# Elementwise steps of a mixer on VectorE and ScalarE in place of GpSimd, and a planner that models the port

## The chip, the cores and the metric

The kernel runs on one core of a Trainium2 chip. The core has a matrix engine (TensorE, PE in the profile; its weight loads are PEld), three elementwise engines (VectorE = DVE, ScalarE = ACT, GpSimd = POOL) and SyncE (SP), which here issues all DMAs. The metric is the device time of one execution in microseconds, the median of several runs.

## The reference

Two layers work on one sequence of 256 tokens by 1024 channels, all in float32. Each layer adds four blocks to x, every one with a norm ahead and a norm behind: a half-weighted SwiGLU feed-forward, a mixer of three branches, a cross-attention into 256 memory tokens, and a second half-weighted feed-forward.

```python
for l in range(DEPTH):
    x = x + 0.5 * _rmsnorm(_swiglu(_rmsnorm(x, ng[0]), w_ffn_in[l, 0], w_ffn_out[l, 0]), ng[1])
    y = _mixer_block(_rmsnorm(x, ng[2]), cos, sin, ...)
    x = x + _rmsnorm(y, ng[3])
    y = _mem_attn(_rmsnorm(x, ng[4]), _rmsnorm(mem, mem_norm[l]), ...)
    x = x + _rmsnorm(y, ng[5])
    x = x + 0.5 * _rmsnorm(_swiglu(_rmsnorm(x, ng[6]), w_ffn_in[l, 1], w_ffn_out[l, 1]), ng[7])
```

The mixer projects its input once, runs causal latent attention with a rotary part (`_mla_branch`), gated linear attention (`_gla_branch`) and RWKV-7 (`_rwkv_branch`), multiplies each branch's projection by a sigmoid gate, adds the three and projects the sum:

```python
merged = gates[:, :, 0] * y_a + gates[:, :, 1] * y_b + gates[:, :, 2] * y_c
return merged @ w_out
```

## The kernel before

**Products in three passes.** The large matmuls use a split of float32: a weight chunk of 128 x 512 is loaded by DMA into one of three `raw` buffers, ScalarE copies its high part into one of eight `whi` buffers, VectorE subtracts to get the low part into `wlo` (`split`), and TensorE makes three products (`mm3`) of high and low parts. The activations are split in the same way into the heap `heapr`. So each weight chunk needs one ScalarE and one VectorE instruction before TensorE can use it. Results gather in eight PSUM banks, two each of `b_g`, `b_ya`, `b_yb` and `b_s`.

**An order that a planner writes.** The program is first recorded as a list of operations (`Program.add`). `order` then plans it: each operation has a cost in us by its engine and shape (`cost`), each dependency a lag, and `forward` goes through the engines in simulated time and takes for each the ready operation of the lowest rank. `backward` derives new ranks from the plan's times, and this is repeated four times; the whole recording is repeated six times with buffers placed by the previous plan's times, and the plan with the shortest simulated span is issued. So a new cost or a new rule in `forward` can change the order of every engine's queue in every part of the kernel, and where buffers lie. On the chip each engine runs its queue strictly in the issued order.

`forward` charges tensor operations a drain when the size of the used part of the array changes (`part` gives the size and place of each matmul's part), and charges half the cost to every second one of the matmuls in a row on different parts of the same size. It knows nothing of an exclusion between VectorE and GpSimd.

**Where GpSimd works.** All of these go through `tt` with GpSimd as engine, or call it directly:

- `rwkv_keys` and `rwkv_products`: 12 products of 128 x 256 a layer, between the projections and the first matmuls of the RWKV chunks.
- `rwkv_front`: four copies of 64 x 256 of the identity into the matrix `MM`, for each half of the tokens.
- `mla_up`: the rotary steps of queries and keys (`rope`), six small steps each, for each half.
- `gla_attend`: a loop over seven levels (chunks of 64, 32, ... 1) and a last step. Each level subtracts on VectorE, takes the exponential on ScalarE, multiplies the key half (128 x 256) and twice the query half into the matrix `zq` (64 x 256 each), and then TensorE multiplies the two; the result goes into the attention matrix by a copy of ScalarE or a predicated copy of VectorE. At the end come two products of 128 x 512 for each half, with the norm's gain and the gate.
- `rwkv_out`: two products or sums with the norm's weight and bias and one with the bonus, 128 x 512, for each half.
- `branch`: four sums of 128 x 512 into the merged result for each of the second and third branches.
- Norms (`meansq`, `rstd`): a scale-and-add and a power, on 128 x 1 to 128 x 8; they stay there. In `ffn` GpSimd also multiplies the gain vector by 0.5.

The triangular solve (`rwkv_solve`) runs on VectorE, 62 small steps in a row for each half, and then goes out to DRAM and back through the buffers `sx` and `si` before `rwkv_back` can start on TensorE. The second half's solve is recorded just ahead of `gla_attend`, and the planner interleaves the two.

Of the kernel before, what the change touches and what calls it, by code (L numbers as in the profile page):

```python
# [16 lines left out]
AF = mybir.ActivationFunctionType  # L17
# [10 lines left out]
EPS = 1e-6  # L28
# [20 lines left out]
class Program:  # L49
# [138 lines left out]

    @staticmethod
    def columns(op):  # L190
        if op[1] == "transpose":
            return op[2][1].shape[0] * np.prod(op[2][1].shape[1:]) / 128
        x = op[3]["rhs"]
        return x.shape[0] * np.prod(x.shape[1:]) * (1 if x.dtype == F32R else 4) / 128
# [6 lines left out]
    def order(self):  # L201

        self.preds = self.graph()
        ops = self.ops
        n = len(ops)
        self.eng = [o[0].name for o in ops]
        self.costs = [self.cost(o) for o in ops]
        self.succ = [[] for _ in range(n)]
        for i, p in enumerate(self.preds):
            for j in p:  # L210
                self.succ[j].append(i)
        self.size = [o[2][0].nbytes() / self.DMA_RATE if o[0].name == "sync" else 0.0 for o in ops]
        self.cols = [self.columns(o) if o[0].name == "tensor" else 0.0 for o in ops]
        self.parts = [self.part(o) for o in ops]
        rank, rest = [0.0] * n, 0.0
        for i in range(n - 1, -1, -1):
            rank[i] = -self.costs[i] + min((rank[s] - self.lag(i, s) for s in self.succ[i]), default=0.0)
        for i in range(n - 1, -1, -1):
            rest += self.costs[i] if self.eng[i] == "tensor" else 0.0
            rank[i] -= self.ALPHA * rest  # L220
        best = None
        for _ in range(self.ROUNDS):
            span, at, order = self.forward(rank)
            if best is None or span < best[0]:
                best = (span, at, order)
            rank = self.backward(at)
        self.span, self.at, order = best
        for i, users in enumerate(self.users):
            t = self.at[i]
            for b in users:  # L230
                b.start, b.end = min(b.start, t[0]), max(b.end, t[1] + (4.0 if self.eng[i] == "sync" else 0.2))
        return order
# [41 lines left out]
    def forward(self, rank):  # L274
# [12 lines left out]
        at = [None] * n  # L287
        parts, size, place, shared = self.parts, (128, 128), None, False
        while len(order) < n:
            best = None  # L290
            for e in names:
# [4 lines left out]
                if t is not None and (best is None or t < best[0]):  # L296
                    best = (t, e)
            t, e = best
            while wait[e] and wait[e][0][0] <= t:
                i = heapq.heappop(wait[e])[1]  # L300
                heapq.heappush(ready[e], (rank[i], i))
# [11 lines left out]
            if e == "tensor":  # L313
                while recent and recent[0][0] < t - self.TICK:
                    recent.popleft()
                if cols[i] < 1500 * cost[i] and sum(x[1] for x in recent) + cols[i] < self.KEEP:
                    j = min((x for x in ready[e] if cols[x[1]] >= 1500 * cost[x[1]]), default=None)
                    if j:
# [3 lines left out]
                        i = j[1]  # L322
                if parts[i][0] != size:
                    j = min((x for x in ready[e] if parts[x[1]][0] == size and x[0] < rank[i] + self.STAY), default=None)
                    if j:
                        ready[e].remove(j)
                        heapq.heapify(ready[e])
                        heapq.heappush(ready[e], (rank[i], i))
                        i = j[1]
                recent.append((t + cost[i], cols[i]))  # L330
            c = cost[i]
            if e == "tensor":
                if parts[i][0] != size:
                    size, shared = parts[i][0], False
                    c += self.DRAIN
                elif size != (128, 128) and not shared and any(
                        a != b for a, b, s in zip(parts[i][1], place, size) if s < 128):
                    shared = True
                    c *= 0.5
                else:  # L340
                    shared = False
                place = parts[i][1]
# [5 lines left out]
            if e == "tensor":  # L348
# [4 lines left out]
                columns += cols[i]  # L353
                c *= 1 if warm else 2
            at[i] = (t, t + c)
            free[e] = t + c
# [89 lines left out]
class Trunk:  # L446
# [369 lines left out]

    def meansq(self, halves, jk, ss):

        for hf in range(2):
            self.act(jk[:, hf * 512:hf * 512 + 512], halves[hf], AF.Square, scale=1.0 / 32, accum_out=ss[:, hf:hf + 1])  # L820
        g = self.nc.gpsimd
        g.tensor_scalar(ss[:, 0:1], ss[:, 0:1], ss[:, 1:2], EPS, ADD, ADD)
        g.tensor_tensor(ss[:, 0:1], ss[:, 0:1], self.mhalf, ALU.pow)
# [19 lines left out]

    def postnorm(self, y, gb, t):

        jk, yg, ss = self.h.alloc(D), self.h.alloc(D), self.sm.alloc(2)
        self.meansq(y, jk, ss)
        for hf, c in enumerate(self.halves):
# [12 lines left out]
    def ffn(self, l, i, st, post_g, nxt, after_first=None):  # L861
# [46 lines left out]
        for c in range(1, NCH):  # L908
# [3 lines left out]
            if c == NCH - 4:  # L912
                gb = self.gain(post_g)
                self.nc.gpsimd.tensor_scalar(gb.ap, gb.ap, 0.5, 1.0, MULT, MULT)
                nxt(None)
# [10 lines left out]
        for t in range(2):  # L926
            for hf in range(2):
                mms(t, hf, NCH - 2, w9)
                mms(t, hf, NCH - 1, w10)
            self.postnorm(ys[t], gb, t)  # L930
            nxt(t)
# [70 lines left out]
    def rwkv_keys(self, l):  # L1002
# [34 lines left out]
        for hp in range(4):  # L1037
            self.tt(kmv[:, hp, :], kmv[:, hp, :], k0[:, hp, :], MULT, nc.gpsimd)
        h.free(self.k0)
        for hp in range(4):  # L1040
            self.tt(aa[:, hp, :], aa[:, hp, :], kv[:, hp, :], MULT, nc.gpsimd)

    def rwkv_products(self, l):
# [5 lines left out]
        for hp in range(4):  # L1049
            self.tt(rv[:, hp, :], self.rr.v(f, b=4)[:, hp, :], self.km.v(f, b=4)[:, hp, :], MULT, nc.gpsimd)  # L1050
        self.bon = self.sm.alloc(16)
# [32 lines left out]
    def rwkv_front(self, l, t):  # L1084
# [6 lines left out]
        mm5 = MM.v("p (c h e n) -> p c h e n", c=2, h=4, e=2)  # L1091
        for u in range(0, 16, 4):
            nc.gpsimd.tensor_copy(MM.v("p (u n) -> p u n", n=128)[0:64, u:u + 4, 0:64],
                                  self.ident[0:64, 0:64].unsqueeze(1).to_broadcast([64, 4, 64]))
        for e in range(2):
# [153 lines left out]
    def rwkv_out(self, l, och, ocl):  # L1249
# [7 lines left out]
        for t in range(2):  # L1257
# [10 lines left out]
            self.tt(y, y, s.ap.unsqueeze(2).to_broadcast([128, 8, 64]), MULT)  # L1268
            self.tt(Y.ap, Y.ap, lw, MULT, nc.gpsimd)
            self.tt(Y.ap, Y.ap, lb, ADD, nc.gpsimd)  # L1270
            bo = self.bon[:, t * 8:t * 8 + 8]
            vn = VN.v(v8, h=8)
            self.tt(vn, vn, bo.unsqueeze(2).to_broadcast([128, 8, 64]), MULT)
            self.tt(Y.ap, Y.ap, VN.ap, ADD, nc.gpsimd)
            ps = self.bank("ya")
# [13 lines left out]

    def rope(self, dst, x1, x2, t, n, eng):  # L1290
        h = self.h
# [4 lines left out]
        for j, (a, b) in enumerate(((x1, c), (x2, s), (x1, s), (x2, c))):  # L1296
            self.tt(tv[:, j], a, b, MULT, eng)
        self.tt(dst[:, :, 0:16], tv[:, 0], tv[:, 1], SUB, eng)
        self.tt(dst[:, :, 16:32], tv[:, 2], tv[:, 3], ADD, eng)
        h.free(T)  # L1300
# [40 lines left out]
    def mla_up(self, l):  # L1341
# [6 lines left out]
        for t in range(2):  # L1348
# [6 lines left out]
            q = qn[t].v(q3, h=8)  # L1355
            self.rope(q[:, :, 64:96], q[:, :, 64:80], q[:, :, 80:96], t, 8, nc.gpsimd)
        wk = self.wload([(0, self.kview(self.w["mla_w_ukv"][l]))], True)[0]
        pr = self.bank("s")[0:32, 0:256]
        for t in range(2):
            kr = sm.alloc(32)  # L1360
            cr = c0[t].ap
            self.rope(kr.ap.unsqueeze(1), cr[:, 384:400].unsqueeze(1), cr[:, 400:416].unsqueeze(1), t, 1, nc.gpsimd)
            self.tr(pr[:, t * 128:t * 128 + 128], kr.ap)
# [98 lines left out]
    def gla_attend(self, l, obh, obl):  # L1462
# [48 lines left out]
        for i, L in enumerate((64, 32, 16, 8, 4, 2, 1)):  # L1511
# [8 lines left out]
            self.act(T.ap, T.ap, AF.Exp)  # L1520
            self.tt(tv[:, :, 0, :], tv[:, :, 0, :], kv[:, :, 0, :], MULT, nc.gpsimd)
            upat = "p (u b x n) -> p u b x n"
            tq, qq = (b.v(upat, u=4, x=2, n=L)[:, :, :, 1, :] for b in (T, QG))
            by_head(Z, lambda pe, z: self.tt(z.rearrange("p u (b n) -> p u b n", n=L), tq[pe], qq[pe], MULT, nc.gpsimd))
            ps = self.bank("yb", (4, 128))
# [7 lines left out]
            else:  # L1533
# [8 lines left out]
        self.act(T.ap, T.ap, AF.Exp)  # L1542
        self.tt(t2[:, :, 0:128], t2[:, :, 0:128], kg[:, :, 0:128], MULT, nc.gpsimd)
        by_head(Z, lambda pe, z: self.tt(z.rearrange("p (h x) n -> p h x n", h=2),
                                         t2[pe, :, 128:256].rearrange("p h (x n) -> p h x n", x=2),
                                         qg[pe, :, 128:256].rearrange("p h (x n) -> p h x n", x=2), MULT, nc.gpsimd))
        ps = self.bank("yb", (2, 256))
# [5 lines left out]
        for t in range(2):  # L1553
# [12 lines left out]
            self.tt(ov, ps, ss.ap.unsqueeze(2).to_broadcast([128, 4, 128]), MULT)  # L1566
            self.tt(ov, ov, self.p_gn.unsqueeze(1).to_broadcast([128, 4, 128]), MULT, nc.gpsimd)
            self.tt(O.ap, O.ap, gg[t].ap, MULT, nc.gpsimd)
            pt = self.bank("yb", (4, 128))
# [13 lines left out]
    def mixer(self, l, st, post_g, nxt):  # L1583
# [33 lines left out]
        def branch(i, o, gt):  # L1617
            for ch in range(2):
                cc = slice(ch * 512, ch * 512 + 512)

                def consume(t, ps):
                    self.tt(gt[t][:, cc], gt[t][:, cc], ps, MULT)
                    if i:
                        self.tt(mg[t][:, cc], mg[t][:, cc], gt[t][:, cc], ADD, nc.gpsimd)

# [216 lines left out]
```

## Time and profile before

| what | value |
|---|---|
| time, median of 3 runs | 1686.76 us (1681.28 to 1687.56) |
| the profiled execution | 1683.41 us, its span 1681.7 us |
| VectorE busy | 1105.1 us |
| ScalarE busy | 964.1 us |
| GpSimd busy | 268.4 us in 383 instructions |
| granted TensorE clock, mean | 0.983 |

Almost every instruction stands on one line of the kernel, that of `issue`, so groups are told apart by their tiles: `b_g` and so on for the PSUM banks, `raw`, `whi` and `wlo` for weight chunks, `heap` and `heapr` for the activations, `small` for norm factors, `zq` for the query half of a GLA level. Spans of an engine are the times from start to end of an instruction, so an instruction that is held up by another engine at the memory shows as a long one, not as idle time. "Idle before" is the time that an engine waited ahead of a group, with who ended the wait.

### The profile page before, as it was taken

The numbers are of one execution on the slowest core, as the hardware profiler recorded it, in microseconds if no ns is written. First come the engines' busy times: TensorE is split into PE (matmuls) and PEld (weight loads), VectorE is DVE, ScalarE is ACT, GpSimd is POOL, SyncE is SP. The second block draws the span as 40 slices with busy tenths as digits, with TensorE's granted clock in tenths as the row PEclk, the third lists the DMA queues.
The fourth block names the chain that finished last, engine by engine and source line by source line (L and its number), as shares of the span: only waits on it lengthen the run. The fifth ranks groups of instructions, "written<-read, shape, count | busy, mean of one in ns | idle before, by whom it ended". The sixth has DMA issues, their size and how long they took to land. (4 is left out here: it accounts for less than half of the span.)

```text
span 1681.7 us, 23946 instructions
## 1 busy us (share of the span) xinstructions
PE 1602.7 (95%) x8623; PEld 1337.0 (80%) x8623; DVE 1105.1 (66%) x1954; ACT 964.1 (57%) x1887; POOL 268.4 (16%) x383
## 2 busy tenths in 40 slices
PE   7999999998899999999999999999978999999998
PEld 5788798776677987888878887887766789878886
DVE  5555656958876667555675557676786776575555
ACT  5455675866445556555555556867854455564544
POOL 7000113105331101000010002310163320010000
PEclk9999999999999999999999999999988999999999
DMA  8655542522555635656555554443225555455652
GB/s 253 207 190 186 171 155 88 169 73 103 170 192 180 206 128 163 202 173 214 174 180 199 193 182 146 131 143 115 91 83 173 175 188 165 149 169 182 199 177 100
DMA packets 206091, 274.91 MB, mean 163 GB/s; under 512 B 28148, under 2 KB 157650, under 8 KB 205972
## 3 DMA queue, kind: packets, MB, share of 16 engines
q1 hardware_dynamic: 205972, 273.39, 50.0%
q8 instruction: 67, 1.10, 0.3%
q14 instruction: 52, 0.43, 0.1%
HBM read 270.60 MB, written 2.75 MB: 163 GB/s over the span
## 5 line engine op out<-in xcount | busy, mean ns | idle before, releaser
L384 DVE TENSOR_TENSOR wlo<-raw,whi 128x512 fp32r<-128x512 f32 (+1 forms) x964 | 673.5, 714 | 401.1 <-ACT whi L384 389.7
L384 ACT CAST whi<-raw 128x512 fp32r<-128x512 f32 (+1 forms) x964 | 582.4, 619 | 484.7 <-PE b_g L384 256.8
L384 PE MATMUL b_g<-whi,heapr 128*128 128x512 f32 (+2 forms) x1904 | 656.3, 405 | 15.8 <-DVE heap L384 5.5
L384 PEld LDWEIGHTS b_g<-whi,heapr 128*128 128x128 f32 x1904 | 357.4, 191 | 97.6 <-DVE heapr L384 7.3
L384 PE MATMUL b_g<-wlo,heapr 128*128 128x512 f32 (+2 forms) x952 | 369.3, 403 | 0.5 <-DVE wlo L384 0.4
L384 PEld LDWEIGHTS b_g<-wlo,heapr 128*128 128x128 f32 x952 | 181.5, 191 | 36.6 <-DVE wlo L384 2.3
L384 PE MATMUL b_g<-heapr,whi 128*128 128x256 f32 x1104 | 201.6, 290 | 2.8 <-DVE heap L384 2.8
L384 POOL TENSOR_SCALAR small<-small 128x1 f32<-128x1 f32 (+2 forms) x52 | 30.3, 583 | 987.4 <-ACT heap L384 962.7
L384 PE MATMUL b_ya<-whi,heapr 128*128 128x512 f32 x480 | 178.0, 394 | 0.2 <-ACT heapr L384 0.2
L384 PE MATMUL b_yb<-whi,heapr 128*128 128x512 f32 x480 | 174.6, 392 | 0.0
L384 PE MATMUL b_s<-whi,heapr 128*128 128x512 f32 x448 | 174.5, 399 | 0.0
L384 PEld LDWEIGHTS b_g<-heapr,whi 128*128 128x128 f32 x1104 | 166.2, 193 | 6.5 <-DVE heap L384 4.0
L384 POOL TENSOR_TENSOR heap<-heap 128x256 f32<-128x256 f32 (+2 forms) x85 | 101.8, 1208 | 207.7 <-DVE heap L384 105.5
L384 PE MATMUL b_g<-heapr,wlo 128*128 128x256 f32 x552 | 134.9, 290 | 0.0
L384 DVE TENSOR_TENSOR heap<-heap 128x512 f32<-128x512 f32 (+31 forms) x296 | 116.6, 406 | 15.8 <-PE b_yb L384 8.8
L384 PEld LDWEIGHTS b_yb<-whi,heapr 128*128 128x128 f32 x480 | 89.8, 188 | 18.9 <-DVE heapr L384 0.2
L384 PEld LDWEIGHTS b_ya<-whi,heapr 128*128 128x128 f32 x480 | 89.3, 188 | 19.2 <-ACT heapr L384 0.4
L384 PE MATMUL b_s<-ident,heap 128*128 128x128 f32 (+2 forms) x449 | 92.7, 275 | 10.1 <-DVE heap L384 8.4
L384 ACT CAST heapr<-b_s 128x256 fp32r<-128x256 f32 (+2 forms) x148 | 65.5, 444 | 58.2 <-PE b_s L384 50.8
L384 PEld LDWEIGHTS b_s<-whi,heapr 128*128 128x128 f32 x448 | 83.6, 188 | 18.4 <-DVE heap L384 0.6
L384 PEld LDWEIGHTS b_g<-heapr,wlo 128*128 128x128 f32 x552 | 96.2, 193 | 1.7 <-issue 1.0
L384 DVE TENSOR_TENSOR heapr<-b_s,heapr 128x256 fp32r<-128x256 f32 (+2 forms) x148 | 75.3, 509 | 33.6 <-ACT heapr L384 33.1
(163 smaller groups left out, 1692.3 us busy)
## 6 DMA issues: line engine op xcount, KB each, us to landing
raw<-in_w_ffn_in_dram SPq DMA_DIRECT2D x172, 512.0 KB, 4.9
raw<-in_w_in_dram SPq DMA_DIRECT2D x50, 1024.0 KB, 5.0
raw<-in_w_ffn_out_dram SPq DMA_DIRECT2D x44, 1024.0 KB, 6.9
raw<-in_mem_wkv_dram SPq DMA_DIRECT2D x16, 1024.0 KB, 6.0
raw<-in_w_branch_dram SPq DMA_DIRECT2D x12, 1024.0 KB, 5.3
raw<-in_w_out_dram SPq DMA_DIRECT2D x8, 1024.0 KB, 5.0
raw<-in_mem_wq_dram SPq DMA_DIRECT2D x8, 1024.0 KB, 4.8
raw<-in_mem_wo_dram SPq DMA_DIRECT2D x8, 1024.0 KB
```

The costliest lines, as they stand in the source:

```text
L384: getattr(eng.real, method)(*a, **k)
```

## The change

The products and sums listed above leave GpSimd for VectorE, by dropping the engine argument (`rope` loses its parameter). The four identity copies of `rwkv_front` become one ScalarE copy of 64 x 1024. The halving of the feed-forward's norm is done inside the norm: the root mean square is taken of twice the values (`over=2`), so that its inverse is half as large, and the multiplication of the gain falls away. In the planner, `shared` marks the operations that read SBUF through what VectorE and GpSimd share, and `forward` lets neither run on it while the other holds it; and for matmuls on parts of the array it prefers one on another place than the last, and charges half the cost to every one on another place.

```diff
     @staticmethod
+    def shared(op):
+
+        eng, method, a, k = op
+        if eng.name not in ("vector", "gpsimd") or method in ("memset", "iota"):
+            return False
+        out = k["out"] if "out" in k else a[0]
+        ins = [x for x in list(a) + list(k.values()) if isinstance(x, bass.AP) and x is not out and x.space != PSUM]
+        ins = [x for x in ins if int(np.prod(x.shape[1:])) > 1]
+        return len(ins) >= (2 if eng.name == "vector" else 1) or eng.name == "gpsimd"
...
+        held = dict(vector=0.0, gpsimd=0.0)
...
+            if e == "gpsimd" and t < held["vector"]:
+                free[e] = held["vector"] + 0.03
+                continue
...
-                if parts[i][0] != size:
-                    j = min((x for x in ready[e] if parts[x[1]][0] == size and x[0] < rank[i] + self.STAY), default=None)
+                if parts[i][0] != size or size != (128, 128) and parts[i][1] == place:
+                    some = [x for x in ready[e] if parts[x[1]][0] == size and x[0] < rank[i] + self.STAY]
+                    j = min((x for x in some if parts[x[1]][1] != place), default=None)
+                    if not j and parts[i][0] != size:
+                        j = min(some, default=None)
...
-                elif size != (128, 128) and not shared and any(
-                        a != b for a, b, s in zip(parts[i][1], place, size) if s < 128):
-                    shared = True
+                elif place != parts[i][1]:
                     c *= 0.5
...
+            if e == "vector" and self.port[i]:
+                t = max(t, held["gpsimd"])
+            if e in held and self.port[i]:
+                held[e] = t + c
...
-    def meansq(self, halves, jk, ss):
+    def meansq(self, halves, jk, ss, over=1):
...
-            self.act(jk[:, hf * 512:hf * 512 + 512], halves[hf], AF.Square, scale=1.0 / 32, accum_out=ss[:, hf:hf + 1])
+            self.act(jk[:, hf * 512:hf * 512 + 512], halves[hf], AF.Square, scale=over / 32, accum_out=ss[:, hf:hf + 1])
...
-        g.tensor_scalar(ss[:, 0:1], ss[:, 0:1], ss[:, 1:2], EPS, ADD, ADD)
+        g.tensor_scalar(ss[:, 0:1], ss[:, 0:1], ss[:, 1:2], EPS * over * over, ADD, ADD)
...
-                self.nc.gpsimd.tensor_scalar(gb.ap, gb.ap, 0.5, 1.0, MULT, MULT)
...
-        for u in range(0, 16, 4):
-            nc.gpsimd.tensor_copy(MM.v("p (u n) -> p u n", n=128)[0:64, u:u + 4, 0:64],
-                                  self.ident[0:64, 0:64].unsqueeze(1).to_broadcast([64, 4, 64]))
+        nc.scalar.copy(MM.v("p (u n) -> p u n", n=128)[0:64, :, 0:64], self.ident[0:64, 0:64].unsqueeze(1).to_broadcast([64, 16, 64]))
...
-            self.tt(Y.ap, Y.ap, lw, MULT, nc.gpsimd)
-            self.tt(Y.ap, Y.ap, lb, ADD, nc.gpsimd)
+            self.tt(Y.ap, Y.ap, lw, MULT)
+            self.tt(Y.ap, Y.ap, lb, ADD)
...
-            self.tt(tv[:, :, 0, :], tv[:, :, 0, :], kv[:, :, 0, :], MULT, nc.gpsimd)
+            self.tt(tv[:, :, 0, :], tv[:, :, 0, :], kv[:, :, 0, :], MULT)
...
-            by_head(Z, lambda pe, z: self.tt(z.rearrange("p u (b n) -> p u b n", n=L), tq[pe], qq[pe], MULT, nc.gpsimd))
+            by_head(Z, lambda pe, z: self.tt(z.rearrange("p u (b n) -> p u b n", n=L), tq[pe], qq[pe], MULT))
...
-                        self.tt(mg[t][:, cc], mg[t][:, cc], gt[t][:, cc], ADD, nc.gpsimd)
+                        self.tt(mg[t][:, cc], mg[t][:, cc], gt[t][:, cc], ADD)
```

The other places (`rwkv_keys`, `rwkv_products`, `rope` and its callers, the last step and the end of `gla_attend`, the third step of `rwkv_out`) change in the same way.

More of the change, by code (lines that the diff above doesn't have):

```diff
@@ L189, in columns @@
     @staticmethod
+    def shared(op):
[6 more added lines that the diff above has]
+        return len(ins) >= (2 if eng.name == "vector" else 1) or eng.name == "gpsimd"
+    @staticmethod
     def columns(op):
@@ L214, in order @@
         self.parts = [self.part(o) for o in ops]
+        self.port = [self.shared(o) for o in ops]
         rank, rest = [0.0] * n, 0.0
@@ L287, in forward @@
         at = [None] * n
-        parts, size, place, shared = self.parts, (128, 128), None, False
+        parts, size, place = self.parts, (128, 128), None
+        held = dict(vector=0.0, gpsimd=0.0)
         while len(order) < n:
@@ L333, in forward @@
                 if parts[i][0] != size:
-                    size, shared = parts[i][0], False
+                    size = parts[i][0]
                     c += self.DRAIN
-                elif size != (128, 128) and not shared and any(
-                        a != b for a, b, s in zip(parts[i][1], place, size) if s < 128):
-                    shared = True
+                elif place != parts[i][1]:
                     c *= 0.5
-                else:
-                    shared = False
                 place = parts[i][1]
@@ L842, in prenorm, with postnorm @@
             self.sm.free(ss)
-    def postnorm(self, y, gb, t):
+    def postnorm(self, y, gb, t, over=1):
         jk, yg, ss = self.h.alloc(D), self.h.alloc(D), self.sm.alloc(2)
-        self.meansq(y, jk, ss)
+        self.meansq(y, jk, ss, over)
         for hf, c in enumerate(self.halves):
@@ L929, in ffn @@
                 mms(t, hf, NCH - 1, w10)
-            self.postnorm(ys[t], gb, t)
+            self.postnorm(ys[t], gb, t, 2)
             nxt(t)
@@ L1037, in rwkv_keys @@
         for hp in range(4):
-            self.tt(kmv[:, hp, :], kmv[:, hp, :], k0[:, hp, :], MULT, nc.gpsimd)
+            self.tt(kmv[:, hp, :], kmv[:, hp, :], k0[:, hp, :], MULT)
         h.free(self.k0)
         for hp in range(4):
-            self.tt(aa[:, hp, :], aa[:, hp, :], kv[:, hp, :], MULT, nc.gpsimd)
+            self.tt(aa[:, hp, :], aa[:, hp, :], kv[:, hp, :], MULT)
     def rwkv_products(self, l):
@@ L1049, in rwkv_products @@
         for hp in range(4):
-            self.tt(rv[:, hp, :], self.rr.v(f, b=4)[:, hp, :], self.km.v(f, b=4)[:, hp, :], MULT, nc.gpsimd)
+            self.tt(rv[:, hp, :], self.rr.v(f, b=4)[:, hp, :], self.km.v(f, b=4)[:, hp, :], MULT)
         self.bon = self.sm.alloc(16)
@@ L1273, in rwkv_out @@
             self.tt(vn, vn, bo.unsqueeze(2).to_broadcast([128, 8, 64]), MULT)
-            self.tt(Y.ap, Y.ap, VN.ap, ADD, nc.gpsimd)
+            self.tt(Y.ap, Y.ap, VN.ap, ADD)
             ps = self.bank("ya")
@@ L1287, in rwkv_out, with rope @@
         sm.free(self.bon)
-    def rope(self, dst, x1, x2, t, n, eng):
+    def rope(self, dst, x1, x2, t, n):
         h = self.h
@@ L1296, in rope @@
         for j, (a, b) in enumerate(((x1, c), (x2, s), (x1, s), (x2, c))):
-            self.tt(tv[:, j], a, b, MULT, eng)
-        self.tt(dst[:, :, 0:16], tv[:, 0], tv[:, 1], SUB, eng)
-        self.tt(dst[:, :, 16:32], tv[:, 2], tv[:, 3], ADD, eng)
+            self.tt(tv[:, j], a, b, MULT)
+        self.tt(dst[:, :, 0:16], tv[:, 0], tv[:, 1], SUB)
+        self.tt(dst[:, :, 16:32], tv[:, 2], tv[:, 3], ADD)
         h.free(T)
@@ L1355, in mla_up @@
             q = qn[t].v(q3, h=8)
-            self.rope(q[:, :, 64:96], q[:, :, 64:80], q[:, :, 80:96], t, 8, nc.gpsimd)
+            self.rope(q[:, :, 64:96], q[:, :, 64:80], q[:, :, 80:96], t, 8)
         wk = self.wload([(0, self.kview(self.w["mla_w_ukv"][l]))], True)[0]
@@ L1361, in mla_up @@
             cr = c0[t].ap
-            self.rope(kr.ap.unsqueeze(1), cr[:, 384:400].unsqueeze(1), cr[:, 400:416].unsqueeze(1), t, 1, nc.gpsimd)
+            self.rope(kr.ap.unsqueeze(1), cr[:, 384:400].unsqueeze(1), cr[:, 400:416].unsqueeze(1), t, 1)
             self.tr(pr[:, t * 128:t * 128 + 128], kr.ap)
@@ L1542, in gla_attend @@
         self.act(T.ap, T.ap, AF.Exp)
-        self.tt(t2[:, :, 0:128], t2[:, :, 0:128], kg[:, :, 0:128], MULT, nc.gpsimd)
+        self.tt(t2[:, :, 0:128], t2[:, :, 0:128], kg[:, :, 0:128], MULT)
         by_head(Z, lambda pe, z: self.tt(z.rearrange("p (h x) n -> p h x n", h=2),
                                          t2[pe, :, 128:256].rearrange("p h (x n) -> p h x n", x=2),
-                                         qg[pe, :, 128:256].rearrange("p h (x n) -> p h x n", x=2), MULT, nc.gpsimd))
+                                         qg[pe, :, 128:256].rearrange("p h (x n) -> p h x n", x=2), MULT))
         ps = self.bank("yb", (2, 256))
@@ L1566, in gla_attend @@
             self.tt(ov, ps, ss.ap.unsqueeze(2).to_broadcast([128, 4, 128]), MULT)
-            self.tt(ov, ov, self.p_gn.unsqueeze(1).to_broadcast([128, 4, 128]), MULT, nc.gpsimd)
-            self.tt(O.ap, O.ap, gg[t].ap, MULT, nc.gpsimd)
+            self.tt(ov, ov, self.p_gn.unsqueeze(1).to_broadcast([128, 4, 128]), MULT)
+            self.tt(O.ap, O.ap, gg[t].ap, MULT)
             pt = self.bank("yb", (4, 128))
```

## The prediction

> **What bounds the kernel now.** First the page: busy shares, then its row of the granted TensorE clock.
>
> ```profile
> span 1681.7 us, 23946 instructions
> ...
> PE 1602.7 (95%) x8623; PEld 1337.0 (80%) x8623; DVE 1105.1 (66%) x1954; ACT 964.1 (57%) x1887; POOL 268.4 (16%) x383
> ...
> PEclk9999999999999999999999999999988999999999
> ```
>
> TensorE is busy in 95% of the span, so time can leave only where it idles or runs at a lower clock, or where its matmuls become denser. Next, the busy times by stage (columns: stretch, its length, then busy us and instructions of PE, PEld, DVE, ACT and POOL, then the granted clock, DMA share, GB/s). The first layer's mixer lies in 260 to 640, the second's in 1080 to 1460.
>
> ```profile
> 260.00:380.00 120.00, 112.20 (x787) 94.84 (x787) 89.40 (x196) 81.03 (x178) 23.62 (x39) 0.99 0.40 121
> 380.00:460.00 80.00, 64.99 (x315) 52.55 (x314) 68.75 (x133) 45.08 (x75) 39.80 (x37) 0.91 0.39 126
> 460.00:640.00 180.00, 178.71 (x1111) 154.07 (x1111) 117.59 (x179) 96.59 (x190) 29.59 (x26) 1.00 0.51 175
> 640.00:1020.00 380.00, 378.57 (x1716) 308.57 (x1715) 233.12 (x386) 206.52 (x396) 12.63 (x17) 1.00 0.58 188
> ...
> 1080.00:1200.00 120.00, 111.08 (x778) 94.74 (x777) 89.17 (x194) 80.13 (x172) 18.92 (x27) 0.96 0.36 111
> 1200.00:1300.00 100.00, 80.98 (x437) 66.56 (x436) 75.83 (x144) 58.15 (x96) 42.36 (x39) 0.90 0.42 134
> 1300.00:1460.00 160.00, 159.07 (x941) 137.40 (x941) 107.93 (x163) 86.70 (x170) 27.30 (x25) 1.00 0.51 171
> ```
>
> Outside two stretches TensorE hardly idles: 1.4 us of the 380 after the first mixer. In 380:460 and 1200:1300, where the gated linear attention and the second triangular solve run, it idles 15.0 and 19.0 us, and its clock falls to 0.91 and 0.90. The clock costs about 0.09 x 65.0 = 5.8 and 0.10 x 81.0 = 8.1 us of work. Together 47.9 us: this is what the change can touch, beside some 17 idle us in 260:380 and 1080:1200.
>
> Now who ends TensorE's idle time there: the waits of 380:460 first, then those of 1200:1300 (columns: total us, times, longest).
>
> ```profile
> PE b_yb L384 <- DVE heap L384: 8.3, 3, 6.0
> PE b_yb L384 <- POOL zq L384: 6.1, 5, 4.5
> ...
> PE b_yb L384 <- DVE heap L384: 5.2, 2, 3.7
> PE b_ya L384 <- DMA heap<-sx: 4.1, 1, 4.1
> PE b_g L384 <- DVE heap L384: 4.0, 2, 2.7
> ...
> PE b_yb L384 <- POOL zq L384: 3.9, 1, 3.9
> ```
>
> Of it, 27.5 us wait for GpSimd's `zq` products or for VectorE. The timeline shows why VectorE is late:
>
> ```profile
> 390.93 4.79 POOL L384 TENSOR_TENSOR heap<-heap 128x256 f32<-128x256 f32 x1 [33.71 <-ACT heap L384]
> ...
> 395.68 1.51 POOL L384 TENSOR_TENSOR zq<-heap 64x256 f32<-64x256 f32 x2
> ...
> 397.25 2.08 PE L384 MATMUL b_yb<-zq,heap 128*128 128x128 f32 x8 [4.46 <-POOL zq L384]
> ...
> 439.32 4.18 POOL L384 TENSOR_TENSOR heap<-heap 128x512 f32<-128x512 f32 x3
> ...
> 439.82 3.76 DVE L384 TENSOR_TENSOR heap<-heap 128x80 f32<-128x80 f32 x3
> ...
> 447.18 0.45 PE L384 MATMUL b_yb<-ident,heap 128*128 128x128 f32 x1 [6.00 <-DVE heap L384]
> ```
>
> At 390.9 one GpSimd product takes 4.79 us while VectorE works without a pause, and TensorE waits 4.46 for what follows. At 439.3 it is the other way round: three GpSimd products run for 4.18 us, and three small solve steps of VectorE need 3.76. Then its queue is behind by that much and TensorE idles 6.00. The two engines exclude each other.
>
> **The change part by part.**
>
> *1. Products and sums move from GpSimd to VectorE.* GpSimd's prices, then VectorE's for like shapes, then VectorE's weight split in a stretch without GpSimd work (80:200), in 380:460 and in 1215:1285 (columns: count, busy us, mean ns, idle before):
>
> ```profile
> L384 POOL TENSOR_TENSOR heap<-heap 128x512 f32<-128x512 f32 x32 | 50.0, 1567 | 104.8 <-DVE heap L384 100.7 <-DMA heap<-in_rwkv_ln_b_dram 3.4
> L384 POOL TENSOR_TENSOR heap<-heap 128x256 f32<-128x256 f32 x40 | 43.3, 1100 | 102.9 <-ACT heap L384 91.2 <-DVE heap L384 4.8 <-issue 4.8
> L384 POOL TENSOR_TENSOR zq<-heap 64x256 f32<-64x256 f32 x32 | 27.2, 849 | 1.2
> L384 POOL TENSOR_TENSOR heap<-heap,pb 128x512 f32<-128x512 f32 x4 | 5.8, 1440 | 1.6 <-DVE heap L384 1.6
> ...
> L384 DVE TENSOR_TENSOR heap<-heap,b_g 128x512 f32<-128x512 f32 x24 | 16.3, 679 | 8.0 <-PE b_g L384 8.0
> L384 DVE TENSOR_TENSOR heap<-b_ya,mask 64x256 f32<-64x256 f32 x32 | 13.4, 419 | 0.4
> ...
> L384 DVE TENSOR_TENSOR wlo<-raw,whi 128x512 fp32r<-128x512 f32 x83 | 56.4, 691 | 46.7 <-ACT whi L384 45.8
> ...
> L384 DVE TENSOR_TENSOR wlo<-raw,whi 128x512 fp32r<-128x512 f32 x33 | 27.7, 842 | 4.4 <-ACT whi L384 4.4
> ...
> L384 DVE TENSOR_TENSOR wlo<-raw,whi 128x512 fp32r<-128x512 f32 x29 | 22.8, 800 | 0.2 <-ACT whi L384 0.2
> ```
>
> VectorE gains 36 x 0.68 + 72 x 0.42 = 54.7 us over both layers, and 48 small rope steps of at most 0.42 each, 20 at most. In one attention stretch it is 24 x 0.42 + 7 x 0.68 = 14.8 us (eight levels of three products, four products of the attention's output, and the three steps of the first half's RWKV output), where 380:460 leaves it 11.2 free. But the blocking goes: 33 x (0.842 - 0.691) = 5.0 us on its splits, and 3 us or so at each knot like the one at 439. So the work just fits, and its chain shortens: one level now runs 1.10 + 2 x 0.85 = 2.8 us on GpSimd (6.3 at the knot at 390.9), and would run 3 x 0.42 = 1.3 on VectorE. At 390.9 the saved 5 us exceed the wait of 4.46. At 439 three products of 0.68 take the place of a block of 4.18, so about 2 of the 6.00 stay. I take three quarters of the 27.5 us, 20.6. The clock lost 13.9 us beside 34.0 idle; I let half of that share go too: 20.6 x 13.9 / 34.0 / 2 = 4.2. Term: **-25**. Bounds: from -13 (only the `zq` waits, 6.1 + 3.9, with 3 of the clock) to -48 (all of it). What comes late next is the landing of the solve's result (the 4.1 us row), which stays, and the exponentials of ScalarE.
>
> In 260:380 and 1080:1200 the keys, the products and the rope move. There TensorE waits for GpSimd only at the rope:
>
> ```profile
> PE b_yb L384 <- POOL heap L384: 2.4, 2, 1.6
> ...
> PE b_yb L384 <- POOL heap L384: 2.5, 2, 1.4
> ```
>
> Term: **-3**, two thirds of it; bounds 0 and -7 with half of the clock's 0.04 x 111 us in 1080:1200. In 460:640 and 1300:1460 the eight branch sums and the second half's RWKV output move: 11 x 0.68 = 7.5 us a layer, beside 62 and 52 us in which VectorE is free and a TensorE that is over 99% busy. Nothing; without that cover 7.5 a layer at most. No step issues a DMA, so SP's queue keeps its work.
>
> *2. The identity goes to ScalarE*, as one 64x1024 copy for four of GpSimd's.
>
> ```profile
> L384 ACT COPY heap<-b_s 32x1024 f32<-32x1024 f32 x4 | 3.9, 1001 | 0.1
> ```
>
> Four of about 1.0 us, beside a ScalarE busy 81 of 120 us: nothing, 4 us without cover. The gain's halving leaves GpSimd for a scale of the norm, in stretches where TensorE hardly idles: nothing.
>
> *3. The planner.* That it knows the exclusion sets the order of all engines anew, in the feed-forward stretches as well. I take 0, with 6 us each way as an estimate: nine splits of 0.69 that come in time or late. The alternation of half arrays:
>
> ```profile
> L384 PE MATMUL b_ya<-heap 64*128 64x128 f32 x256 | 29.9, 285 | 0.6 <-ACT heap L384 0.2
> ...
> 1174.76 1.71 PE L384 MATMUL b_ya<-heap 64*128 64x128 f32 x16
> ```
>
> That is 0.117 us each on average, 0.107 where packed, against 2.08 / 8 = 0.26 for the full-array products at 397.25. They overlap already; packing all saves 256 x 0.010 = 2.6 us. Term: **-1**, bounds 0 and -3. The Trainium skill, "TensorEngine Tiling (Array Packing)", section "Theoretical Speedup", allows up to twofold for a dimension of at most 64. By it, applied to the 29.9 us, this term would be -15; the rows say the factor is already there.
>
> **Sum.** -25 - 3 - 1 = -29. The profiled run took 1683.4 (span 1681.7), which gives 1654; the median of the runs is 3.3 higher, so 1658.
>
> **The rivals.** *VectorE takes GpSimd's place as the bound* (no change). For it speaks how full it is in the middle of the attention:
>
> ```profile
> 400.00:420.00 20.00, 17.93 (x92) 14.65 (x92) 19.76 (x29) 11.27 (x20) 15.93 (x18) 0.91 0.16 54
> 420.00:440.00 20.00, 17.71 (x91) 14.36 (x91) 19.27 (x37) 10.11 (x18) 11.61 (x11) 1.00 0.49 171
> ```
>
> One of 40 us is free. GpSimd does 27.5 of its 39.8 us there, so about 10 us of the 14.8 land here. If little blocking is in VectorE's busy time, the splits slip by 10 us a layer, and 29 - 20 = 9 remain: 1678. Against it speak the splits' 842 ns. The Trainium skill's "Perfetto Trace Analysis", section "Optimizing Scalar/DVE Operations", says that the two engines share a port, so that shifting work between them might not help. That is this rival; the 4.18 us knot rather shows the shared port as a loss that goes.
>
> *VectorE waits in order for ScalarE* (slower). GpSimd could afford to wait for the exponential; on VectorE everything behind the waiting product waits too, the weight splits first. ScalarE changes tables six times in 380:460:
>
> ```profile
> L384 ACT ACT_TABLE_LOAD x6 | 7.7, 1283 | 0.1
> ```
>
> With a table load and a copy of 0.6 ahead of it a level stalls 2 to 3 us; eight levels in each of two layers at 3 us are 48. It decides from 37 us on, 2.3 a level: then the 29 are gone and 8 more. Time at 48: 1687 + 19 = 1706. Against it: the order can set other work between a subtraction and its product, and VectorE waits little there now (4.4 us for ScalarE in 33 splits).
>
> *All of it goes*: 47.9 + 5 us and the splits' ease: 1634, if the planner now hits the real times.
>
> **How the numbers follow.** Forecast (1645 to 1674): 59%. VectorE as the bound: 17%. Waits in order: 12%. All of it: 12%. The range 1632 to 1692 leaves out the slower case and the far end of the last. About 0.5% (8.4 us) is what a measurement can tell from no change: faster 0.71, within 0.17, slower 0.12.
>
> **What would show it.** Right: POOL's busy time falls by at least the 126 us of the four rows, splits in the attention near 0.69 us, PE idle in the two stretches from 34 to under 15 us, clock there over 0.95. Wrong: VectorE idle on ScalarE's `heap` before products; PE waits on `wlo`; half arrays far under 0.107; idle time in the feed-forward stretches, which only the new order can bring.

## The result and the profile after

The changed kernel takes 1642.9 us (median of its runs) against 1685.8 of the kernel before, measured beside it: a ratio of 0.974, 95% interval 0.972 to 0.977, so 43 us or 2.6% faster. The forecast was 29 us faster, 1658, with 1632 to 1692 as its range. One of its four executions, at a granted TensorE clock of 0.75 instead of 0.99, took 1956.8 us and is left out of the ratio. The profiled execution has a span of 1641.1 us.

The page after: busy shares, then the granted TensorE clock by slices.

```profile
span 1641.1 us, 23827 instructions
...
PE 1591.3 (97%) x8623; PEld 1330.6 (81%) x8623; DVE 1102.5 (67%) x2110; ACT 967.3 (59%) x1889; POOL 113.2 (7%) x207
...
PEclk9999999999999999999999999999999999999999
```

TensorE does the same 8623 matmuls. Its idle time fell from 79.0 to 49.8 us, and its busy time by 11.4 us, with a mean granted clock of 0.990 instead of 0.983. GpSimd lost 155 us of work, and yet VectorE, which took most of it over, is busy for 2.6 us less. The same view by stages as in the prediction, of the changed kernel:

```profile
260.00:380.00 120.00, 113.23 (x793) 95.11 (x794) 93.80 (x237) 83.33 (x180) 2.43 (x3) 0.99 0.40 125
380.00:460.00 80.00, 78.63 (x392) 64.74 (x391) 75.47 (x176) 55.12 (x89) 8.58 (x6) 1.00 0.49 166
460.00:640.00 180.00, 177.26 (x1098) 153.79 (x1098) 116.51 (x190) 99.10 (x200) 12.57 (x18) 0.98 0.50 167
640.00:1020.00 380.00, 374.98 (x1694) 305.03 (x1693) 233.23 (x388) 205.95 (x396) 14.69 (x21) 1.00 0.57 188
...
1080.00:1200.00 120.00, 116.39 (x818) 98.70 (x817) 93.09 (x228) 89.93 (x188) 1.48 (x2) 1.00 0.40 124
1200.00:1300.00 100.00, 96.60 (x539) 77.39 (x538) 84.73 (x186) 54.96 (x99) 13.97 (x12) 0.97 0.53 171
```

In 380:460 and 1200:1300 together TensorE idles 4.8 us instead of 34.0, and the lower clock costs 0.03 x 96.6 = 2.9 us instead of 13.9. VectorE is fuller than before, 75.5 of 80 us in place of 68.8. A window does not hold the same work in both kernels, since the second layer begins about 15 us earlier; the landing of the first layer's second solve moved just past 460, where 2.3 of the 2.7 idle us of 460:640 lie, and the granted clock of 460:480 is 0.83 now. So the first stretch is better taken up to 480 (before, then after):

```profile
380.00:480.00 100.00, 84.39 (x487) 68.34 (x486) 80.83 (x150) 54.76 (x96) 45.44 (x42) 0.93 0.43 141
...
380.00:480.00 100.00, 96.33 (x546) 79.56 (x545) 83.96 (x189) 62.21 (x104) 9.45 (x8) 0.97 0.51 171
```

With 1200:1300, TensorE's idle time fell from 34.6 to 7.1 us, and the clock's cost from 14.0 to 5.8: 36 of the 43 us. The waits of TensorE in the two stretches (380:460, then 1200:1300) show that what was waited for in both is nearly gone:

```profile
PE b_yb L403 <- DVE heap L403: 0.7, 1, 0.7
PE b_yb L403 <- DVE zq L403: 0.5, 2, 0.3
...
PE b_ya L403 <- DMA heap<-sx: 1.4, 1, 1.4
PE b_yb L403 <- DVE heap L403: 0.6, 1, 0.6
PE b_yb L403 <- DVE zq L403: 0.6, 2, 0.3
```

The timeline at the first two levels of the attention, where GpSimd had needed 6.3 us:

```profile
389.51 0.75 DVE L403 TENSOR_TENSOR heap<-heap 128x256 f32<-128x256 f32 x2
390.19 0.84 DVE L403 TENSOR_TENSOR zq<-heap 64x256 f32<-64x256 f32 x2
...
391.60 1.05 PE L403 MATMUL b_yb<-zq,heap 128*128 128x128 f32 x8
391.74 0.84 DVE L403 TENSOR_TENSOR zq<-heap 64x256 f32<-64x256 f32 x2
...
392.94 1.06 PE L403 MATMUL b_yb<-zq,heap 128*128 128x128 f32 x8
```

The two 64x256 products take 0.84 us together, and TensorE starts the second level 1.34 us after the first (the third only at 397.19).

### The profile page after: what moved, and what is told of

Same layout as the page of the kernel before. It is cut to its first block, busy times and chain, and to the rows that moved or that the text cites. A ratio compares the mean times of both kernels' runs of the same rounds, so it can differ in the third digit from the quotient of the medians.

```text
span 1641.1 us, 23827 instructions
## 1 busy us (share of the span) xinstructions
PE 1591.3 (97%) x8623; PEld 1330.6 (81%) x8623; DVE 1102.5 (67%) x2110; ACT 967.3 (59%) x1889; POOL 113.2 (7%) x207
## 4 chain that ended last, share of the span: by engine, by line
PE 79%; DVE 10%; ACT 5%; DMA 3%; issue 2%; SPq 0%; DVEq 0%; POOLq 0%; ACTq 0%; POOL 0%
PE b_g L403 42%; PE b_ya L403 15%; PE b_s L403 11%; PE b_yb L403 10%; DVE heap L403 5%; DVE wlo L403 3%; ACT heap L403 3%; DMA raw<-in_w_ffn_in_dram 1%; ACT whi L403 1%; DMA raw<-in_w_ffn_out_dram 1%; ACT L403 1%; DVE heapr L403 1%; DVE small L403 1%; DVE x L403 1%; DMA si<-heap 0%
## 5 line engine op out<-in xcount | busy, mean ns | idle before, releaser
L403 DVE TENSOR_TENSOR wlo<-raw,whi 128x512 fp32r<-128x512 f32 (+1 forms) x964 | 648.7, 688 | 382.7 <-ACT whi L403 370.8
L403 PE MATMUL b_g<-wlo,heapr 128*128 128x512 f32 (+2 forms) x952 | 365.3, 398 | 3.1 <-DVE wlo L403 3.1
L403 DVE TENSOR_TENSOR heap<-heap 128x256 f32<-128x256 f32 (+29 forms) x376 | 130.9, 364 | 11.3 <-ACT heap L403 5.9
L403 POOL TENSOR_SCALAR small<-small 128x1 f32<-128x1 f32 (+2 forms) x52 | 34.3, 659 | 1276.2 <-ACT heap L403 1109.7
L403 PE MATMUL b_ya<-wlo,heapr 128*128 128x512 f32 x240 | 92.9, 392 | 0.0
```

What stands on the lines that cost most here:

```text
L403: getattr(eng.real, method)(*a, **k)
```

## The experiments

Two theories stood against each other after the result. EXCLUSION: GpSimd and VectorE held each other up, and the time is gone as soon as the products leave GpSimd. PLAN: the order of all queues is what became better. The change does both at once, so the runs take it apart. An order means here all that a plan fixes, the buffers' places included. Differences below are against the kernel before, run beside each on the same chip (medians 1685.1 to 1685.3).

**1. The old order, the new engine.** The program is recorded and planned as before, with the products as GpSimd's; only at the issue they go to VectorE. The queues of TensorE, ScalarE and SyncE keep their order word for word.

```diff
         for i in order:
             eng, method, a, k = self.ops[i]
-            getattr(eng.real, method)(*a, **k)
+            getattr((self.vector if i in self.moved else eng).real, method)(*a, **k)
```

> The plan of the kernel before, order of all queues kept; only the engine that executes the moved products and sums is VectorE instead of GpSimd (identity copies and the gain's halving stay on GpSimd). Theory EXCLUSION (the time before was lost because GpSimd and VectorE block each other, and goes as soon as the products leave GpSimd, whatever the plan): 1650 to 1662, with the splits in the second half of the attention back near 0.69 us. Theory PLAN (the gain comes from a planner that knows the port, and a good order): 1678 or more, since this order was made for two engines side by side.

1672.4 us, ratio 0.992 (0.990 to 0.995): 13 us. That lies between both expectations. The two stretches by stage, then the splits in them:

```profile
380.00:460.00 80.00, 70.11 (x402) 56.82 (x402) 70.14 (x168) 49.72 (x83) 5.54 (x6) 0.96 0.44 142
...
1200.00:1300.00 100.00, 84.34 (x488) 67.38 (x487) 79.76 (x182) 58.13 (x98) 7.21 (x8) 0.97 0.45 144
```

```profile
L385 DVE TENSOR_TENSOR wlo<-raw,whi 128x512 fp32r<-128x512 f32 x36 | 24.6, 687 | 5.1 <-ACT whi L385 4.9
...
L385 DVE TENSOR_TENSOR wlo<-raw,whi 128x512 fp32r<-128x512 f32 x40 | 27.3, 685 | 9.0 <-ACT whi L385 8.2 <-PE b_s L385 0.6
```

The splits are back at 0.69 us, so the holding-up is gone. Yet TensorE still idles 9.9 + 15.7 = 25.6 us there, of 34.0. The timeline at the place of the former wait of 6.00 us says why:

```profile
442.14 2.69 DVE L385 TENSOR_TENSOR heap<-heap 128x72 f32<-128x72 f32 x9
444.75 0.69 DVE L385 TENSOR_TENSOR wlo<-raw,whi 128x512 fp32r<-128x512 f32 x1
445.36 0.69 DVE L385 TENSOR_TENSOR heapr<-b_yb,heapr 128x512 fp32r<-128x512 f32 x1
...
446.10 0.33 PE L385 MATMUL b_yb<-ident,heap 128*128 128x128 f32 x1 [1.87 <-DVE heapr L385]
```

Nine elementwise steps stand in a row ahead of a weight split and of the split that TensorE waits for. That order was written for two engines side by side. The wait is 1.87 us instead of 6.00, as the prediction left about 2 there. But TensorE waits for the attention's own products as long as before, though they are VectorE's now (waits of TensorE, 380:460, then 1200:1300):

```profile
PE b_yb L385 <- DVE zq L385: 6.2, 5, 1.7
...
PE b_yb L385 <- DVE zq L385: 3.5, 5, 0.9
```

In the kernel before the same products of GpSimd had cost 6.1 and 3.9 us of waiting. That it is the old order that sets other work ahead of them is an inference from the runs below.

**2. The old engines, the new planner.** Only `shared`, its use in `forward` and the alternation are added to the kernel before.

> The kernel before with the new planner alone (port model and alternation); all products and sums stay on GpSimd. EXCLUSION: the blocking itself stays, the order only goes around it: 1670 to 1682, splits in the attention still over 0.75 us. PLAN: 1650 or less, most of the 43 us.

1656.7 us, ratio 0.983 (0.981 to 0.985): 28 us, without moving one product. The splits in 380:460 and 1200:1300 are as slow as ever:

```profile
L403 DVE TENSOR_TENSOR wlo<-raw,whi 128x512 fp32r<-128x512 f32 x38 | 31.4, 840 | 2.9 <-ACT whi L403 2.7
...
L403 DVE TENSOR_TENSOR wlo<-raw,whi 128x512 fp32r<-128x512 f32 x46 | 36.1, 798 | 8.2 <-ACT whi L403 8.0
```

0.840 and 0.798 us: the blocking is all there, but 38 splits come through in 380:460 where there were 33. TensorE's idle time fell by 18 us in 380:480 and 1200:1300, and by 10 us in 260:380 and 1080:1200. EXCLUSION alone falls with this run.

**3. The new order, the old engine.** The mirror image of the first: planned as the changed kernel (TensorE, ScalarE and SyncE in its order), but the products go to GpSimd at the issue.

```diff
-            getattr(eng.real, method)(*a, **k)
+            getattr((self.gpsimd if i in self.moved else eng).real, method)(*a, **k)
```

> The plan of the changed kernel, order of TensorE, ScalarE and SyncE kept, but the moved products and sums are executed by GpSimd. The other way round (the old order with VectorE) gave 13 us of the 43. If order and engine each give their own part: 1656 or so, 13 above 1643. If the new order holds only because a product takes 0.4 instead of 1.1 us and blocks nobody: 1670 or more, with VectorE's splits in the attention over 0.75 us.

1662.1 us, ratio 0.987 (0.985 to 0.989): 23 us faster than before, 19 slower than the changed kernel, and between both expectations. The splits take 0.73 us in 380:460 and 0.82 in 1200:1300. With the first run this makes a table of two by two:

| | products on GpSimd | products on VectorE |
|---|---|---|
| order of before | 1685 | 1672 |
| order of after | 1662 | 1643 |

The engine is worth 13 to 19 us in a fixed order, the order 23 to 30 with a fixed engine. (The lower row also has the identity on ScalarE and no halving of the gain, so the order's part includes these two.) Both are needed for the 43, and the order is the larger part. PLAN alone falls too.

**4. The planner's rules one by one, on the kernel before.** First the port model without the alternation, then the alternation without the port model.

> The kernel before with the port model alone in the planner, no alternation, all work where it was. The new planner as a whole gave 1656.7 on the old engines. Theory PORT (the port model gives these 28 us, since it sets the other engine's work out of the way): 1650 to 1662. Theory REDRAW (any new plan draws another time, with no meaning): anywhere from 1660 to 1690.

1670.0 us, ratio 0.992 (0.990 to 0.994), 15 us: about half of the planner's 28, outside PORT's range and inside REDRAW's.

> The kernel before with the alternation alone. PORT: 1680 to 1688, no change beyond the 3 us that I gave it. REDRAW, or an alternation that is worth more than I thought: 1675 or less.

1676.7 us, ratio 0.996 (0.994 to 0.998), 8 us: between both expectations. The half-array products of this run:

```profile
L383 PE MATMUL b_ya<-heap 64*128 64x128 f32 x256 | 27.5, 293 | 0.9 <-DVE heap L383 0.6 <-ACT heap L383 0.2
```

They became 29.9 - 27.5 = 2.4 us denser, as the bound of 2.6 said. The other 6 us are idle time that the new order leaves out elsewhere (72.4 us of TensorE's span in place of 79.0). The rule does not make these products denser in every order: in the run of the whole planner above they take 32.0 us.

**5. Is any new order a draw?** One constant of the ranks is changed, which has no meaning for the work: `ALPHA` from 0.10 to 0.11, in the kernel before and in the changed one.

> The kernel before with one constant of the ranks changed (ALPHA 0.11 for 0.10), which means nothing but gives another order. PORT: within 8 us of 1685. REDRAW: off by 10 or more either way.

1684.1 us, ratio 0.999 (0.997 to 1.001).

> The changed kernel with the same constant changed (ALPHA 0.11 for 0.10). PORT: 1638 to 1650; with GpSimd out of the way the time hardly hangs on the plan. REDRAW: off by 10 or more from 1643 either way.

1644.6 us, ratio 0.977 (0.975 to 0.979) to the kernel before, 2 us above the changed one. Two redraws moved the time by 1 and 2 us, so 15 and 28 us are hardly luck of the draw. The first changed TensorE's order as much as the port model did: in its trace 73% of the positions in the queue hold the same kind of instruction as in the kernel before, with the port model alone 76%. For the 8 us of the alternation two draws are a thin measure.

**6. The moves without the rules.** First the changed kernel with `shared` always false, then without the alternation, then with the planner of before, which has neither.

> The changed kernel with a planner that does not know the port (no operation is marked as sharing it). EXCLUSION: only the norms' small GpSimd steps are left to collide, so 1640 to 1650. PLAN: 1660 or more.

1643.0 us, ratio 0.975 (0.973 to 0.976): as the changed kernel.

> The changed kernel with the planner's old rule for matmuls on parts of the array (no alternation, half the cost for every second one). My prediction's step: worth 0 to 3 us, so 1641 to 1648, as far as a new order doesn't bring its own shift. If the alternation is a main part of the gain: 1655 or more, and the 256 products on 64 rows back at 29.9 us from 28.6.

1639.9 us, ratio 0.973 (0.971 to 0.975): 3 us less than the changed kernel, with intervals that overlap. The products on 64 rows take 31.7 us in it, against 28.6 in the changed kernel, and the time does not show it.

> All moved work of the changed kernel (products and sums on VectorE, the identity on ScalarE, no halving of the gain), planned by the planner of before. So far: the new planner without the moves 1656.7, the moves without the port model 1643.0, without the alternation 1639.9. Theory MOVES (the moves with any new plan give all of it, and the planner's new rules give time only while the products are on GpSimd): 1638 to 1650. Theory BOTH (each of the two rules can stand in for the other, but one is needed): 1655 or more.

1650.7 us, ratio 0.980 (0.978 to 0.983): 35 of the 43 us, a hair outside the first range and far from the second. Once the products are on VectorE, either rule can be missing; without both, 8 us stay behind. No run shows why either rule is enough. So the moves themselves bring most of the new order: the old planner, too, writes another order when it is told that the products are VectorE's, and that order is 22 us better than the old one with the products on VectorE (1672.4 in the first run, where the identity stays on GpSimd).

**7. Which moves.** With the new planner, only the attention's products move (`gla_attend`), then everything but them.

> New planner; only the products of the gated linear attention move to VectorE (52 products and the 8 at its output over both layers), everything else stays on GpSimd. My prediction's step, 25 of 29 us by the attention: 1642 to 1648, against 1656.7 with the planner alone. If the gain lies in the keys, the rope and the sums: 1652 or more.

1641.1 us, ratio 0.974 (0.972 to 0.976): the whole gain, 2 us below the changed kernel with overlapping intervals. (By the trace 48 products move and the 8 at the output, not 52 and 8.) The splits still take 0.77 us in 380:480 and 0.79 in 1200:1300, since the rest of GpSimd's products still collide with them; so the slow splits by themselves cost no time that shows.

> The changed kernel with the attention's products still on GpSimd. My prediction's step: 1651 to 1658, near the planner alone. If the other moves carry the gain: 1647 or less.

1649.4 us, ratio 0.979 (0.978 to 0.981): 36 us, between both expectations. Against the planner alone (28) the attention adds 16 and the rest 7, and both together 14: the parts are not a sum. No run beats the changed kernel clearly.

## Why the prediction came out as it did

**The place was right.** The term for the attention and the second solve held most of the gain: over 380:480 and 1200:1300, 27.6 us of idle time and 8.2 us of clock went, 36 us. The marks that it named came: GpSimd's busy time fell by 155 us (at least 126 forecast), the idle time of 34 is under 15, the clock there 1.00 and 0.97 (0.97 in both when the first is taken up to 480), and the splits of 380:460 and 1200:1300 are at 0.69:

```profile
L403 DVE TENSOR_TENSOR wlo<-raw,whi 128x512 fp32r<-128x512 f32 x44 | 30.0, 685 | 0.2
...
L403 DVE TENSOR_TENSOR wlo<-raw,whi 128x512 fp32r<-128x512 f32 x49 | 33.4, 686 | 4.4 <-ACT whi L403 4.0
```

**The size of that term was too small**: -25, with three quarters of 27.5 us of named waits and half of the clock. Four fifths of all the idle time there went (34.6 to 7.1), waits outside the 27.5 among it, and more than half of the clock's cost. The wait for the solve's landing mostly stayed, as the prediction said: 5.8 us over the whole kernel before, 3.7 after. The forecast's own range, 1645 to 1674, was missed by 2 us; the time lies nearer to the rival "all of it goes", 1634, than to 1658.

**The step that failed is the planner's, taken at 0 with 6 us each way.** In the second run the new rules are worth 28 us with all engines as before. On top of the moves they are worth 8 (1650.7 to 1642.9), where this term and the alternation's were put at 1 together, 9 at most; and the moves under the old planner are worth 35, where the forecast had 28. Of these 35 the engine gave 13 in the old order; the other 22 come with the new order that the old planner writes for the moves (the identity and the halving included). The prediction read the waits of 4.46 and 6.00 us as the cost of the exclusion and credited them to the engine. In this kernel the exclusion costs in two ways: what it holds up, and that the order made without it was the wrong one, which the port model alone mends by 15 us. That the forecast came as near as 15 us is in part luck: engine and order changed together, and the waits of the trace are the sum of what both can take away.

**VectorE's work was priced right.** 0.42 and 0.68 us were asked, and the changed kernel shows:

```profile
L403 DVE TENSOR_TENSOR zq<-heap 64x256 f32<-64x256 f32 x32 | 13.3, 416 | 0.3
...
L403 DVE TENSOR_TENSOR heap<-heap,pb 128x512 f32<-128x512 f32 x4 | 2.7, 685 | 0.0
```

The second level follows the first after 1.34 us, where 1.3 a level were forecast. The cover was there too: VectorE's total did not grow, since its steps are held up less: the splits alone fell from 673.5 to 648.7 us. The identity's copies on ScalarE take 1.04 us each, as forecast; what they do to the waits was not separated.

**The keys' term**, -3 with -7 as its end: TensorE's idle time in 260:380 and 1080:1200 fell by 6.3 us and the clock of the second from 0.96 to 1.00, past the far end of the term, with the reserve that these windows shift. But the move of the keys and the rope is not shown to be the cause: with the planner alone, and both on GpSimd, the idle time there fell by 10 us, and moving the attention's products alone gave the whole gain.

**The alternation**, -1: 29.9 became 28.6 us of busy time in the changed kernel, and taking the rule out (the run without alternation) costs nothing. But the reading behind the term was wrong. The full-array products at 397.25, at 0.26 us each, ran at a granted clock of 0.50 (397 to 402); the same products at 391.60 of the changed kernel, at a clock of 1.00, take 1.05 / 8 = 0.13. Against that the 0.107 of the packed half arrays is faster by a fifth, not twofold. So no run shows that the twofold gain that the Trainium skill allows for half arrays ("TensorEngine Tiling (Array Packing)", "Theoretical Speedup") was in the kernel already.

**The rivals.** VectorE as the bound: it is full to 94% in 380:460, but TensorE waits 1.2 us for it there. The Trainium skill says ("Perfetto Trace Analysis", "Optimizing Scalar/DVE Operations") that shifting work between these two engines might not help. Here, shifting it *off* GpSimd did help: 13 us in a fixed order. Waits in order for ScalarE: ahead of its `heap` steps VectorE waits 0.2 us for ScalarE in 380:460; the order sets other work between a subtraction and its product. Idle time did come back outside the mixers, 1.4 to 5.0 us in 640:1020, within the 6 allowed.

## What to carry to other kernels

Where a planner or a hand-written order sets queues that run strictly in order, a wait in the trace measures the engine and the order together; to price a move of work, run it once in the old order, and once planned anew. Two engines that exclude each other cost by the blocked time and by the order that did not count on it: here telling the planner of it gave 15 us by itself and 28 with the alternation, taking the products off GpSimd in the old order 13, and all of it 43. When one engine is cleared of a kind of work, the rule that avoided the collision may become dispensable: without the port model the changed kernel takes 1643.0 us, though without both rules 1650.7.

## What the runs showed of the hardware

While VectorE works without a pause, a step of GpSimd can be held up for long. In the changed kernel one of its steps on 4 columns takes 3.52 us, while VectorE runs one step with two inputs in SBUF after the other (timeline, GpSimd first):

```profile
419.74 3.52 POOL L403 TENSOR_SCALAR small<-small 128x4 f32<-128x4 f32 x1 [65.68 <-DVE small L403]
...
419.79 0.69 DVE L403 TENSOR_TENSOR wlo<-raw,whi 128x512 fp32r<-128x512 f32 x1
420.39 0.32 DVE L403 TENSOR_TENSOR heap<-heap 128x160 f32<-128x160 f32 x1
420.63 0.69 DVE L403 TENSOR_TENSOR wlo<-raw,whi 128x512 fp32r<-128x512 f32 x1
...
422.29 0.69 DVE L403 TENSOR_TENSOR wlo<-raw,whi 128x512 fp32r<-128x512 f32 x1
422.89 0.30 DVE L403 TENSOR_TENSOR heap<-heap 128x144 f32<-128x144 f32 x1
423.20 0.69 DVE L403 TENSOR_TENSOR wlo<-raw,whi 128x512 fp32r<-128x512 f32 x1
```

The four steps of this shape take 3.52, 0.76, 5.13 and 0.20 us, 2.40 on average, where they took 0.75 in the kernel before (groups by form, before and then after):

```profile
L384 POOL TENSOR_SCALAR small<-small 128x4 f32<-128x4 f32 x4 | 3.0, 746 | 7.8 <-DVE small L384 7.7
```

```profile
L403 POOL TENSOR_SCALAR small<-small 128x4 f32<-128x4 f32 x4 | 9.6, 2401 | 139.6 <-DVE small L403 139.6
```

VectorE's steps keep their 0.69 and 0.3 us meanwhile, and GpSimd's step ends only as a ninth one starts. The step of 5.13 us, from 1231.36, spans twelve steps of VectorE and ends at 1236.49, just after the last of them (at 1236.43), when VectorE itself stands waiting for that norm, 1.20 us. Not every small step got longer: the 44 of 128x1 take 0.52 us on average, 0.57 before. The Trainium skill ("SBUF — State Buffer", "SBUF: two separate sides") says that the engine that starts first gets the shared port pair and the other one blocks. It leaves open whose turn it is at the next instruction. Here, by these spans, GpSimd was passed over for eight and for twelve steps in a row. VectorE waits 7.4 us in all for GpSimd's norm factors in the changed kernel, 1.5 at the longest, and no wait of a matmul is put down to GpSimd; what such a delay would cost in a norm that the next matmuls wait for is not shown.
